# Raw state-space parameters loaded from GpSimd's queue, their tables begun in the first quarter of the first MLP, and the last gate made inside the second MLP

## The chip, the cores and the metric

One Trainium2 chip, of which the kernel uses one core. The metric is the device time of one execution in microseconds. The core's engines are TensorE (PE: matmuls; PEld is its weight loads), VectorE (DVE), ScalarE (ACT), GpSimd (POOL) and SyncE (SP); each runs its own instructions in a fixed order and waits on semaphores for the others. TensorE's clock has two levels, 1.2 and 2.4 GHz; the granted clock is its mean as a share of the higher one.

## The reference

Two layers on x of 256 tokens and 2048 channels. Each has a token mixer and a squared-ReLU MLP of 8192 hidden channels; before each stands an RMS norm with shift and scale, behind each a gated residual add. The six vectors of a layer come from the conditioning vector c.

```python
for i in range(2):
    mod = silu(c) @ ada_w[i] + ada_b[i]
    sh1, sc1, g1, sh2, sc2, g2 = split(mod, 6)
    h = rmsnorm(x, ln1_g[i]) * (1 + sc1) + sh1
    y = stick_breaking_mixer(h, ...) if i == 0 else s5_mixer(h, ...)
    x = x + g1 * y
    h = rmsnorm(x, ln2_g[i]) * (1 + sc2) + sh2
    a = relu(h @ mlp_w1[i])
    x = x + g2 * ((a * a) @ mlp_w2[i])
```

The S5 mixer runs 128 groups of 16 channels through a complex diagonal state space of 64 states. From lambda, dt, B and C (b_re, b_im, c_re, c_im) it needs discretised matrices and powers of the diagonal: the tables of this text.

## The kernel before

Every large product is f32 and split in two: a weight tile of 512 KB is loaded into w by SP's queue (L128), ACT rounds it to wh (L130), DVE computes the rest wl = w - wh (L132), and PE makes three products, 24 matmuls per tile in the MLP. w, wh and wl have three buffers each, so PE can go on for at most three tiles when DVE stops. After each tile the program calls `tick`, which counts `now`, makes a share (`rate`) of a unit of the vectors from c, and runs what `at` has put down for this tick. A unit is a load of 512 KB into adaw (L265) and two DVE instructions (L350, for the first of a sum L348). `pace` sets the rate so that a vector is done after so many ticks, `drain` finishes it at once.

The first MLP has four quarters of 64 tiles: 32 of w1, then 32 of w2. `between` is called in the first quarter after 16 tiles, `ready` in the last. While this MLP runs, the S5 tables are made: `s5_tables` puts down, for each of eight groups gi, `s5_raws` (loads b_re and b_im into the tile W and c_re, c_im into C, each with one buffer), `s5_powers` (PE turns C over, L896; ACT copies it to CT, L899; POOL, L903 to L917, and DVE, L921 to L926, multiply; POOL's queue stores W to pw in DRAM, L927) and two `s5_turns` (POOL multiplies turns, L744 to L848, and stores it to rot, L849). The S5 mixer loads pw and rot again.

PE and POOL run in the order in which the program is written; the order on SP, ACT and DVE is made by the scheduler when the program is built, and is fixed then. The last vector, g2 of layer 1, stands at the end of the queue of units, and the second MLP reads it in its first residual, 36 tiles in.

```python
w = self.wp.tile([P, a, b], F32, name="w", bufs=self.nw)
nc.sync.dma_start(w, src)
h = self.wp.tile([P, a, b], F32R, name="wh", bufs=self.nh)
nc.scalar.activation(h, w, AF.Copy)
l = self.wp.tile([P, a, b], F32R, name="wl", bufs=self.nh)
nc.vector.tensor_tensor(l, w, h.bitcast(F32), op=OP.subtract)
```

Of the kernel before, what the change touches and what calls it, by code (L numbers as in the profile page):

```python
# [56 lines left out]
class Trunk:  # L57
# [424 lines left out]
            nc.scalar.activation(r[:, j, :S], r[:, j, :S], func, bias=r[:, j, S:])  # L482

    @with_exitstack
    def mlp(ctx, self, layer, nxt=None, last=False, between=None, middle=None):
        nc = self.nc
        w1, w2 = self.i["mlp_w1"][layer], self.i["mlp_w2"][layer]
        hH, hL = self.h()
# [4 lines left out]
        for q in range(4):  # L493
            aH = rp.tile([P, NB, S], F32R, name="aH", bufs=1)
            aL = rp.tile([P, NB, S], F32R, name="aL", bufs=1)
            if q == 0:
# [6 lines left out]
                    nc.scalar.activation(halves[g], acc[:, :, :S + 1], AF.Copy)  # L503
                if between:
                    between()
            if q == 1 and middle:
                middle()
            for g in range(8):
                if 8 * q + g < ahead:
                    acc = self.gemm_cols(w1, q * 2048 + g * 256, hH, hL, 8, 16)  # L510
# [2 lines left out]
                else:  # L513
                    src = self.gemm_cols(w1, q * 2048 + g * 256, hH, hL)
# [297 lines left out]
    def s5_tables(self, tmp):  # L812
        v = self.recorder = Recorder(self.nc.vector)
        lo = tmp.tile([P, 2, 64, 8], F32, name="s5lo")
        hi = tmp.tile([P, 2, 64, 8], F32, name="s5hi")
        t, c2, s2 = (tmp.tile([P, 64], F32, name=n) for n in ("s5t", "c2", "s2"))
        pc, ps = self.s5["pc"], self.s5["ps"]
        tb = tmp.tile([P, 64, 4], F32, name="s5tb")
        for tab in (lo, hi):
            v.memset(tab[:, 0, :, 0:1], 1.0)  # L820
            v.memset(tab[:, 1, :, 0:1], 0.0)
            for n in (1, 2, 4):
                B = lambda a: a[:, :, None].to_broadcast([P, 64, n])
                self.cmul(v, tab[:, 0, :, n:2 * n], tab[:, 1, :, n:2 * n],
                          tab[:, 0, :, 0:n], tab[:, 1, :, 0:n], B(pc), B(ps), tb[:, :, :n])
                self.cmul(v, c2, s2, pc, ps, pc, ps, t)
                pc, c2 = c2, pc
                ps, s2 = s2, ps
        self.rot = [self.dram.tile([P, 3, 4 * 64], F32, name="rot%d" % bi) for bi in range(16)]
        self.pw = [self.dram.tile([P, 2, 2, 4, 8, 16], F32, name="pw%d" % gi) for gi in range(8)]  # L830
        for gi in range(8):
            self.at(28 + 16 * gi, self.s5_raws, tmp, gi)
            self.at(32 + 16 * gi, self.s5_powers, tmp, gi)
            for bi in (2 * gi, 2 * gi + 1):
                self.at(36 + 8 * bi, self.s5_turns, tmp, lo, hi, bi)

    def s5_turns(self, tmp, lo, hi, bi):
        nc = self.nc
# [30 lines left out]
    def s5_raws(self, sp, gi):  # L869
        nc, i = self.nc, self.i  # L870
        g0 = 16 * gi
        W = sp.tile([P, 2, 2, 4, 8, 16], F32, name="W")
        Ec = W[:, 0]
        C = sp.tile([P, 2, 2, 2, 64], F32, name="C", bufs=1)
        for c, n in enumerate(("s5_b_re", "s5_b_im")):
            nc.sync.dma_start(Ec[:, c, 0], i[n][0, g0:g0 + 16].rearrange("(q a) p c -> (a p) q c", a=2))
        for c, n in enumerate(("s5_c_re", "s5_c_im")):
            src = i[n][0, g0:g0 + 16].rearrange("(b g) c p -> (g c) b p", b=2)
            for dup in range(2):
                nc.sync.dma_start(C[:, c, :, dup], src)  # L880
        self.raw = W, C

    def s5_powers(self, sp, gi):
# [244 lines left out]
    def run(self):  # L1128
        nc = self.nc
# [31 lines left out]
        M = lambda i: bool(0 >> i & 1)  # L1161
        self.sums = self.ctx.enter_context(self.tc.tile_pool(name="sums", bufs=1))
        mid = [self.ada_vec(1, 4, M(4)), self.ada_vec(1, 3, M(5))]
        nxt = [self.ada_vec(1, 1, M(1)), self.ada_vec(1, 0, M(2))]
        self.queue += [self.ada_vec(0, 5, M(0))] + nxt + [self.ada_vec(1, 2, M(3))] + mid + [self.ada_vec(1, 5, M(6))]
        self.dram = self.ctx.enter_context(self.tc.tile_pool(name="dram", bufs=1, space=bass.MemoryType.DRAM))
        self.rate = 1.0

        def between():
            self.drain(gates[1])  # L1170
            self.shifts(8, 16, 0, 1)
            for kb in range(8, 16):
                self.fold(kb, 0, 1)
            self.rate = 0.6

        stp = ExitStack()

        def params():
            tmp = stp.enter_context(self.tc.tile_pool(name="s5t", bufs=1))
            self.s5_tables(tmp)  # L1180

        def ready():
            self.recorder.play(None)
# [2 lines left out]
            self.open_h(self.pers)  # L1186
            self.shifts(0, 16, 1, 0)

        self.mlp(0, nxt=ready, between=between, middle=params)
        self.dump("x2")  # L1190
        self.rate = 0.35
        self.s5_mixer(mid)
        self.dump("x3")
        self.logexp()
        self.rate = 1.0
        self.mlp(1, last=True)


# [26 lines left out]
```

## Time and profile before

| | |
|---|---|
| median of 3 runs | 2492.97 us (2491.97 to 2493.75) |
| profiled execution | 2488.38 us |
| its span, first to last instruction | 2486.6 us |
| busy: PE, DVE, ACT, POOL | 2374.3, 1830.0, 1207.1, 255.6 us |
| mean granted TensorE clock | 0.986 |
| DMA, mean | 252 GB/s |

The busy time is a sum over stages that have different limits: attention (to about 490 us), the first MLP (to 1341), the S5 mixer (to about 1730) and the second MLP. A wait in the profile names the instruction that waited, the one that released it, the time in total, the times and the longest. Idle time of an engine that nobody waits for costs nothing.

### The profile page before, as it was taken

To read this page: it belongs to the slowest core of one execution; us is meant where nothing else is said; L and a number is where in the kernel's file an instruction comes from. 1 tells how busy PE (TensorE), PEld (TensorE's weight loads), DVE (VectorE), ACT (ScalarE), POOL (GpSimd) and SP (SyncE) were. 2 spreads that over 40 slices of the span, in tenths; PEclk is the share of its full clock that TensorE was granted. 3 is DMA by queue.
4 is the path that set the end of the run, shared out by engine and by line. 5 is a ranking of instruction groups with operands and counts; after the bars stand their busy time and mean duration, and the time that the engine had idled before them with its cause. 6 is when DMAs were issued, how large, how long until landed. Compare 5 with 4: busy or idle time off the path is not lost.

```text
span 2486.6 us, 48432 instructions
## 1 busy us (share of the span) xinstructions
PE 2374.3 (95%) x19843; PEld 2234.8 (90%) x19843; DVE 1830.0 (74%) x2479; ACT 1207.1 (49%) x1806; POOL 255.6 (10%) x292
## 2 busy tenths in 40 slices
PE   7999999999999888988999999999999999999998
PEld 4776789899999778888999998999999999999998
DVE  5699999999888878787797699658555555555543
ACT  4534875355444234433546676444543543543543
POOL 0000100000003444454400000000000000000000
PEclk9999999999999989999999999999999999999999
DMA  9898899999998888888898577768555655655654
GB/s 337 301 309 301 289 315 320 334 309 317 320 306 286 274 269 276 262 287 282 279 312 304 179 240 228 230 186 280 177 181 186 184 183 185 185 184 184 185 184 140
DMA packets 503058, 627.28 MB, mean 252 GB/s; under 512 B 44434, under 2 KB 374580, under 8 KB 500532
## 3 DMA queue, kind: packets, MB, share of 16 engines
q1 hardware_dynamic: 499776, 609.31, 75.1%
q0 software_dynamic: 2432, 14.68, 1.5%
q8 instruction: 155, 2.54, 0.4%
q14 instruction: 67, 0.55, 0.1%
q10 hardware_dynamic: 628, 0.21, 0.0%
HBM read 607.34 MB, written 16.78 MB: 251 GB/s over the span
## 4 chain that ended last, share of the span: by engine, by line
PE 58%; DVE 13%; issue 10%; DMA 9%; POOL 7%; ACT 2%; SPq 0%; ACTq 0%; DVEq 0%; POOLq 0%
PE acc L159 14%; PE acc L161 14%; PE acc L160 14%; DMA adaw<-in_ada_w 5%; DVE wl L132 4%; PE acc L145 3%; PE acc L146 3%; PE acc L147 3%; DVE adacc L350 3%; DMA rot<-turns 2%; DVE adsums L350 2%; DMA w<-in_mlp_w 2%; PE mp L291 1%; PE mp L322 1%; ACT wh L130 1%
## 5 line engine op out<-in xcount | busy, mean ns | idle before, releaser
L130 ACT ACTIVATE wh<-w 128x1024 fp32r<-128x1024 f32 x736 | 777.5, 1058 | 1052.9 <-PE acc L161 544.6
L132 DVE TENSOR_TENSOR wl<-w,wh 128x1024 fp32r<-128x1024 f32 x736 | 914.9, 1245 | 409.3 <-ACT wh L130 408.3
L159 PE MATMUL acc<-hH,wl 128*128 128x258 f32 (+1 forms) x2816 | 808.1, 287 | 33.7 <-DVE wl L132 32.2
L161 PE MATMUL acc<-hH,wh 128*128 128x258 f32 (+1 forms) x2816 | 799.5, 284 | 0.0
L160 PE MATMUL acc<-hL,wh 128*128 128x258 f32 (+1 forms) x2816 | 798.0, 283 | 0.5 <-DVE hL L122 0.5
L159 PE MATMUL acc<-aH,wl 128*128 128x256 f32 x2048 | 587.4, 287 | 39.1 <-DVE wl L132 38.4
L160 PE MATMUL acc<-aL,wh 128*128 128x256 f32 x2048 | 581.6, 284 | 0.0
L161 PE MATMUL acc<-aH,wh 128*128 128x256 f32 x2048 | 581.6, 284 | 0.0
L159 PEld LDWEIGHTS acc<-hH,wl 128*128 128x128 f32 x2816 | 535.9, 190 | 48.7 <-DVE wl L132 38.3
L160 PEld LDWEIGHTS acc<-hL,wh 128*128 128x128 f32 x2816 | 536.6, 191 | 0.7 <-DVE hL L122 0.7
L161 PEld LDWEIGHTS acc<-hH,wh 128*128 128x128 f32 x2816 | 535.1, 190 | 0.0
L159 PEld LDWEIGHTS acc<-aH,wl 128*128 128x128 f32 x2048 | 391.0, 191 | 48.5 <-DVE wl L132 47.1
L160 PEld LDWEIGHTS acc<-aL,wh 128*128 128x128 f32 x2048 | 391.1, 191 | 0.0
L161 PEld LDWEIGHTS acc<-aH,wh 128*128 128x128 f32 x2048 | 391.0, 191 | 0.0
L350 DVE SCALAR_TENSOR_TENSOR adacc<-adaw,cond,adacc 128x512 f32<-128x512 f32 x390 | 296.9, 763 | 22.5 <-DMA adaw<-in_ada_w 19.2
L350 DVE SCALAR_TENSOR_TENSOR adsums<-adaw,cond,adsums 128x512 f32<-128x512 f32 x270 | 216.1, 802 | 30.5 <-DMA adaw<-in_ada_w 26.5
L145 PE MATMUL acc<-wh,hL 128*128 128x512 f32 x384 | 156.8, 408 | 5.8 <-ACT wh L130 3.1
L146 PE MATMUL acc<-wl,hH 128*128 128x512 f32 x384 | 153.6, 400 | 3.4 <-DVE wl L132 3.3
L147 PE MATMUL acc<-wh,hH 128*128 128x512 f32 x384 | 152.6, 398 | 0.0
L145 PEld LDWEIGHTS acc<-wh,hL 128*128 128x128 f32 x384 | 73.3, 191 | 32.3 <-issue 13.7
L146 PEld LDWEIGHTS acc<-wl,hH 128*128 128x128 f32 x384 | 72.9, 190 | 21.2 <-DVE wl L132 6.3
L147 PEld LDWEIGHTS acc<-wh,hH 128*128 128x128 f32 x384 | 73.0, 190 | 17.0
(288 smaller groups left out, 2068.9 us busy)
## 6 DMA issues: line engine op xcount, KB each, us to landing
w<-in_mlp_w SPq DMA_DIRECT2D x512, 512.0 KB, 3.9
adaw<-in_ada_w SPq DMA_DIRECT2D x384, 512.0 KB, 5.8
w<-in_sb_w_in SPq DMA_DIRECT2D x96, 512.0 KB, 5.5
w<-in_s_w_glu SPq DMA_DIRECT2D x64, 512.0 KB, 3.9
w<-in_sb_w_out SPq DMA_DIRECT2D x32, 512.0 KB, 5.6
w<-in_s_w_in SPq DMA_DIRECT2D x32, 512.0 KB, 4.6
pw<-W POOLq DMA_DIRECT2D x8, 1024.0 KB, 4.2
W<-pw SPq DMA_DIRECT2D x8, 1024.0 KB, 6.7
```

Of the source, the lines that this page charges most:

```text
L130: nc.scalar.activation(h, w, AF.Copy)
L132: nc.vector.tensor_tensor(l, w, h.bitcast(F32), op=OP.subtract)
L145: nc.tensor.matmul(o, aL(kb)[:, s], H[:, kk], start=(kb == k0), stop=False)
L146: nc.tensor.matmul(o, aH(kb)[:, s], L[:, kk], start=False, stop=False)
L147: nc.tensor.matmul(o, aH(kb)[:, s], H[:, kk], start=False, stop=(kb == k1 - 1))
L159: nc.tensor.matmul(o, L[:, kk, s], aH(kb), start=(kb == k0), stop=False)
L160: nc.tensor.matmul(o, H[:, kk, s], aL(kb), start=False, stop=False)
L161: nc.tensor.matmul(o, H[:, kk, s], aH(kb), start=False, stop=(kb == k1 - 1))
L291: nc.tensor.matmul(st["bank"][32 * kk:32 * kk + 32], self.cond32[:, 4 * t + kk], pair[kk // 2][:, kk % 2], start=(t == 0), stop=(t == 3))
L322: nc.tensor.matmul(st["bank"][32 * i:32 * i + 32], self.ones[:, 0:32], acc, start=True, stop=True)
L350: nc.vector.scalar_tensor_tensor(acc, wt[:, kk], c, acc, op0=OP.mult, op1=OP.add)
```

## The change

The six loads of `s5_raws` go from SP's queue to POOL's. `params`, which opens the tables, is called at the end of `between`, 16 tiles into the first MLP, and no longer at the start of its second quarter; a group now takes 22 ticks, with the first turns ahead of the powers, where it took 16, with both turns behind. The rate of the units in the first MLP is 0.5 after `between`, and was 0.6. The last vector leaves the queue and joins it just before the second MLP, at a pace of 29 ticks.

```diff
--- before.py
+++ after.py
@@ -482,7 +482,7 @@
             nc.scalar.activation(r[:, j, :S], r[:, j, :S], func, bias=r[:, j, S:])
 
     @with_exitstack
-    def mlp(ctx, self, layer, nxt=None, last=False, between=None, middle=None):
+    def mlp(ctx, self, layer, nxt=None, last=False, between=None):
         nc = self.nc
         w1, w2 = self.i["mlp_w1"][layer], self.i["mlp_w2"][layer]
         hH, hL = self.h()
@@ -503,8 +503,6 @@
                     nc.scalar.activation(halves[g], acc[:, :, :S + 1], AF.Copy)
                 if between:
                     between()
-            if q == 1 and middle:
-                middle()
             for g in range(8):
                 if 8 * q + g < ahead:
                     acc = self.gemm_cols(w1, q * 2048 + g * 256, hH, hL, 8, 16)
@@ -829,10 +827,11 @@
         self.rot = [self.dram.tile([P, 3, 4 * 64], F32, name="rot%d" % bi) for bi in range(16)]
         self.pw = [self.dram.tile([P, 2, 2, 4, 8, 16], F32, name="pw%d" % gi) for gi in range(8)]
         for gi in range(8):
-            self.at(28 + 16 * gi, self.s5_raws, tmp, gi)
-            self.at(32 + 16 * gi, self.s5_powers, tmp, gi)
-            for bi in (2 * gi, 2 * gi + 1):
-                self.at(36 + 8 * bi, self.s5_turns, tmp, lo, hi, bi)
+            o = 30 + 22 * gi
+            self.at(o, self.s5_raws, tmp, gi)
+            self.at(o + 1, self.s5_turns, tmp, lo, hi, 2 * gi)
+            self.at(o + 9, self.s5_powers, tmp, gi)
+            self.at(o + 14, self.s5_turns, tmp, lo, hi, 2 * gi + 1)
 
     def s5_turns(self, tmp, lo, hi, bi):
         nc = self.nc
@@ -873,11 +872,11 @@
         Ec = W[:, 0]
         C = sp.tile([P, 2, 2, 2, 64], F32, name="C", bufs=1)
         for c, n in enumerate(("s5_b_re", "s5_b_im")):
-            nc.sync.dma_start(Ec[:, c, 0], i[n][0, g0:g0 + 16].rearrange("(q a) p c -> (a p) q c", a=2))
+            nc.gpsimd.dma_start(Ec[:, c, 0], i[n][0, g0:g0 + 16].rearrange("(q a) p c -> (a p) q c", a=2))
         for c, n in enumerate(("s5_c_re", "s5_c_im")):
             src = i[n][0, g0:g0 + 16].rearrange("(b g) c p -> (g c) b p", b=2)
             for dup in range(2):
-                nc.sync.dma_start(C[:, c, :, dup], src)
+                nc.gpsimd.dma_start(C[:, c, :, dup], src)
         self.raw = W, C
 
     def s5_powers(self, sp, gi):
@@ -1162,22 +1161,24 @@
         self.sums = self.ctx.enter_context(self.tc.tile_pool(name="sums", bufs=1))
         mid = [self.ada_vec(1, 4, M(4)), self.ada_vec(1, 3, M(5))]
         nxt = [self.ada_vec(1, 1, M(1)), self.ada_vec(1, 0, M(2))]
-        self.queue += [self.ada_vec(0, 5, M(0))] + nxt + [self.ada_vec(1, 2, M(3))] + mid + [self.ada_vec(1, 5, M(6))]
+        self.queue += [self.ada_vec(0, 5, M(0))] + nxt + [self.ada_vec(1, 2, M(3))] + mid
+        last = self.ada_vec(1, 5, M(6))
         self.dram = self.ctx.enter_context(self.tc.tile_pool(name="dram", bufs=1, space=bass.MemoryType.DRAM))
         self.rate = 1.0
+
+        stp = ExitStack()
+
+        def params():
+            tmp = stp.enter_context(self.tc.tile_pool(name="s5t", bufs=1))
+            self.s5_tables(tmp)
 
         def between():
             self.drain(gates[1])
             self.shifts(8, 16, 0, 1)
             for kb in range(8, 16):
                 self.fold(kb, 0, 1)
-            self.rate = 0.6
-
-        stp = ExitStack()
-
-        def params():
-            tmp = stp.enter_context(self.tc.tile_pool(name="s5t", bufs=1))
-            self.s5_tables(tmp)
+            self.rate = 0.5
+            params()
 
         def ready():
             self.recorder.play(None)
@@ -1186,13 +1187,14 @@
             self.open_h(self.pers)
             self.shifts(0, 16, 1, 0)
 
-        self.mlp(0, nxt=ready, between=between, middle=params)
+        self.mlp(0, nxt=ready, between=between)
         self.dump("x2")
         self.rate = 0.35
         self.s5_mixer(mid)
         self.dump("x3")
         self.logexp()
-        self.rate = 1.0
+        self.queue.append(last)
+        self.pace(29, last)
         self.mlp(1, last=True)
```

DVE, about the first two multiplications of the second group's b (L921 and L922 before, L920 and L921 in the change; a line number of the change is one lower from there on, and `x2` means two equal instructions). Before, the wl ahead of them is the seventh after the transposes of the first group:

```order
L418 SCALAR_TENSOR_TENSOR xT<-half_6164,mod_79,xT 128x256 x2
L132 TENSOR_TENSOR wl<-w,wh 128x1024
L921 TENSOR_TENSOR w_8972<-W,powers 128x384
L922 TENSOR_TENSOR w_8973<-W,powers 128x384
L132 TENSOR_TENSOR wl<-w,wh 128x1024
L923 TENSOR_TENSOR W<-w_8972,w_8973 128x384
L350 SCALAR_TENSOR_TENSOR adsums<-adaw,cond,adsums 128x512
L924 TENSOR_TENSOR w_8972<-W,powers 128x384
L132 TENSOR_TENSOR wl<-w,wh 128x1024
L925 TENSOR_TENSOR w_8973<-W,powers 128x384
```

In the change, again seven tiles after the first group's transposes:

```order
L132 TENSOR_TENSOR wl<-w,wh 128x1024
L920 TENSOR_TENSOR w_7745<-W,powers 128x384
L921 TENSOR_TENSOR w_7746<-W,powers 128x384
L350 SCALAR_TENSOR_TENSOR adsums<-adaw,cond,adsums 128x512
L922 TENSOR_TENSOR W<-w_7745,w_7746 128x384
L350 SCALAR_TENSOR_TENSOR adsums<-adaw,cond,adsums 128x512
L132 TENSOR_TENSOR wl<-w,wh 128x1024
L923 TENSOR_TENSOR w_7745<-W,powers 128x384
L924 TENSOR_TENSOR w_7746<-W,powers 128x384
```

The two instructions keep their distance of seven tiles to the transposes of the group before, and the next wl stands behind them; in the change L922 (formerly L923) and the two instructions of a unit (L350) stand between.

POOL, from the store of the first group's W. Before, two sets of turns follow (the first is shown), and then the next group's powers:

```order
L927 DMA pw_7140<-W 128x2048
L744 TENSOR_TENSOR turnq<-s5lo,s5hi 128x256
L745 TENSOR_TENSOR turns<-s5lo,s5hi 128x256
L746 TENSOR_TENSOR turns<-turnq,turns 128x256
L747 TENSOR_TENSOR turnq<-s5lo,s5hi 128x256
L748 TENSOR_TENSOR turns<-s5lo,s5hi 128x256
L749 TENSOR_TENSOR turns<-turnq,turns 128x256
L848 TENSOR_SCALAR turns<-turns 128x256
L849 DMA rot_7124<-turns 128x768
```

In the change one set follows, and behind its store the loads of the next group:

```order
L926 DMA pw_5475<-W 128x2048
L742 TENSOR_TENSOR turnq<-s5lo,s5hi 128x256
L743 TENSOR_TENSOR turns<-s5lo,s5hi 128x256
L744 TENSOR_TENSOR turns<-turnq,turns 128x256
L745 TENSOR_TENSOR turnq<-s5lo,s5hi 128x256
L746 TENSOR_TENSOR turns<-s5lo,s5hi 128x256
L747 TENSOR_TENSOR turns<-turnq,turns 128x256
L847 TENSOR_SCALAR turns<-turns 128x256
L848 DMA rot_5460<-turns 128x768
L875 DMA W<-in_s_b_re 128x8x16
L875 DMA W<-in_s_b_im 128x8x16
L879 DMA C<-in_s_c_re 128x2x64 x2
```

The loads of b (L875) and C (L879) moved into this queue, behind the store of W and a set of turns.

SP, about the loads of the second group's b. Before:

```order
L128 DMA w<-in_mlp_w 128x4x256
L265 DMA adaw<-in_ada_w 128x2x512
L128 DMA w<-in_mlp_w 128x4x256
L876 DMA W<-in_s_b_re 128x8x16
L128 DMA w<-in_mlp_w 128x4x256
L876 DMA W<-in_s_b_im 128x8x16
L265 DMA adaw<-in_ada_w 128x2x512
L128 DMA w<-in_mlp_w 128x4x256
L265 DMA adaw<-in_ada_w 128x2x512
```

At the same distance from the first group's transposes in the change:

```order
L128 DMA w<-in_mlp_w 128x4x256
L265 DMA adaw<-in_ada_w 128x2x512
L128 DMA w<-in_mlp_w 128x4x256
L265 DMA adaw<-in_ada_w 128x2x512
L128 DMA w<-in_mlp_w 128x4x256
L265 DMA adaw<-in_ada_w 128x2x512
L128 DMA w<-in_mlp_w 128x4x256
L265 DMA adaw<-in_ada_w 128x2x512
```

The two loads of W between the weights are gone; weights and units alternate.

## Rows read from the trace of the kernel before

**Rows 1.** The page: TensorE's busy time, its share of the span and its instructions.
```profile
PE 2374.3 (95%) x19843; PEld 2234.8 (90%) x19843; DVE 1830.0 (74%) x2479; ACT 1207.1 (49%) x1806; POOL 255.6 (10%) x292
```

**Rows 2.** Windows: stretch, length, busy us (x instructions) per engine, clock, DMA share, GB/s.
```profile
541.00:781.00 240.00, 235.94 (x1947) 232.47 (x1946) 213.06 (x296) 120.79 (x151) 0.00 (x0) 1.00 0.94 315
781.00:1197.00 416.00, 355.01 (x2742) 344.86 (x2740) 327.04 (x373) 149.32 (x177) 197.43 (x210) 0.93 0.84 273
1197.00:1341.00 144.00, 138.85 (x1139) 135.33 (x1138) 125.23 (x167) 71.41 (x100) 28.84 (x30) 1.00 0.91 302
1414.00:1514.00 100.00, 100.00 (x1709) 91.81 (x1707) 88.73 (x132) 70.79 (x147) 0.00 (x0) 1.00 0.74 238
1660.00:1730.00 70.00, 70.00 (x587) 69.03 (x586) 58.64 (x83) 31.91 (x41) 0.00 (x0) 1.00 0.84 270
1900.00:2000.00 100.00, 100.00 (x837) 100.00 (x836) 52.33 (x51) 48.87 (x59) 0.00 (x0) 1.00 0.60 182
```

**Rows 3.** The line L896 (transposes of C): ns min/median/max, first and last start.
```profile
L896 PE MATMUL mp<-ident,C x32: 270/272/274, 781.0 to 1197.4; 128*128 128x128 f32 x32
```

**Rows 4.** Timeline of PE, first and fifth group: start us, us, instruction.
```profile
781.04 0.60 PE L896 MATMUL mp<-ident,C 128*128 128x128 f32 x4
...
1023.89 0.60 PE L896 MATMUL mp<-ident,C 128*128 128x128 f32 x4
```

**Rows 5.** Waits of SP's queue, 781 to 1197: us in total, times, longest.
```profile
SPq L876 <- DMA pw<-W: 73.1, 7, 12.3
```

**Rows 6.** Waits, all engines, 781 to 1197 us.
```profile
PEld acc L159 <- DVE wl L132: 69.1, 36, 7.0
```

**Rows 7.** Timeline of POOL, first and fifth group.
```profile
784.64 0.51 POOL L903 TENSOR_TENSOR t<-CT,fr 128x128 f32<-128x128 f32 x1 [389.78 <-ACT CT L899]
...
798.64 0.74 POOL L927 DMA_DIRECT2D pw<-W  x1 [0.31 <-POOL W L917]
...
806.33 0.62 POOL L849 DMA_DIRECT2D rot<-turns  x1 [0.31 <-POOL turns L848]
...
1026.03 0.63 POOL L903 TENSOR_TENSOR t<-CT,fr 128x128 f32<-128x128 f32 x1 [20.30 <-ACT CT L899]
...
1048.00 0.62 POOL L849 DMA_DIRECT2D rot<-turns  x1 [0.30 <-POOL turns L848]
```

**Rows 8.** Timeline of SP, first group.
```profile
803.57 0.37 SPq L876 DMA_DIRECT2D W<-in_s_b_re  x1
```

**Rows 9.** Timeline of DVE, first group; in brackets the idle time before and its releaser.
```profile
802.15 1.64 DVE L132 TENSOR_TENSOR wl<-w,wh 128x1024 fp32r<-128x1024 f32 x1
805.82 0.56 DVE L921 TENSOR_TENSOR w<-W,powers 128x384 f32<-128x384 f32 x1 [2.03 <-DMA W<-in_s_b_re]
809.16 0.56 DVE L922 TENSOR_TENSOR w<-W,powers 128x384 f32<-128x384 f32 x1 [2.78 <-DMA W<-in_s_b_im]
809.64 1.22 DVE L132 TENSOR_TENSOR wl<-w,wh 128x1024 fp32r<-128x1024 f32 x1
...
812.82 0.75 DVE L350 SCALAR_TENSOR_TENSOR adsums<-adaw,cond,adsums 128x512 f32<-128x512 f32 x1 [1.50 <-DMA adaw<-in_ada_w]
```

**Rows 10.** The lines L927, L876 and L128: DMA issues, ns min/median/max.
```profile
L927 POOL DMA_DIRECT2D pw<-W x8: 603/603/738, 798.6 to 1212.8; - x8
...
L876 SPq DMA_DIRECT2D W<-in_s_b_re x8: 367/368/458, 711.4 to 1161.5; - x8
L876 SPq DMA_DIRECT2D W<-in_s_b_im x8: 498/574/578, 711.9 to 1162.5; - x8
...
L128 SPq DMA_DIRECT2D w<-in_mlp_w x512: 367/368/1473, 480.1 to 2465.3; - x171
```

**Rows 11.** Windows of the instructions on adaw alone (DVE's part).
```profile
541.00:1341.00 800.00, 0.00 (x0) 0.00 (x0) 262.95 (x331) 0.97 0.88 291
1197.00:1341.00 144.00, 0.00 (x0) 0.00 (x0) 48.80 (x64) 1.00 0.91 302
1660.00:1730.00 70.00, 0.00 (x0) 0.00 (x0) 23.15 (x32) 1.00 0.84 270
```

## The prediction

> **What bounds the kernel now.** I read the page first: TensorE (PE) is busy 95% of the span [rows 1], so the question is where the rest is lost. The table of windows answers it [rows 2]. A weight tile is 24 matmuls. In the second MLP 837 matmuls pass in 100 us, 100/(837/24) = 2.867 us per tile: PE's own pace. In the first MLP, 541 to 781 us holds 1947 matmuls, or 81.1 tiles in 240 us, 2.96 each; 1197 to 1341 us holds 1139, or 47.5 tiles, 3.03 each; together 2.99. Between them, 781 to 1197 us, it is the stage of the state-space tables that falls out: the granted clock is 0.93 and PE loses 61 us of busy time there alone. The four transposes of C open each group of the tables. Eight groups start between 781.0 and 1197.1 us (the last of the 32 transposes at 1197.4) [rows 3], so seven intervals of 16 tiles took 416 us, 59.4 us each. PE needs 16 x 2.867 + 0.6 (the transposes) = 46.5 us. That is 13 us lost per interval, some 90 us in all.
>
> Then I asked who waits. SP's queue lists 73.1 us in seven waits, up to 12.3 us: the load of b_re into W waits for the store of the group before, because W has one buffer [rows 5]. Behind it stand the weights. This is what the move to GpSimd's queue (POOL) removes. But PE itself waits for wl, which VectorE (DVE) writes [rows 6], and DVE has a wait of its own for the same loads.
>
> Take the first interval and count from its transposes at T0 = 781.04 [rows 4]. POOL starts on the powers at 784.64, issues the store of W at 798.64 and the store of the next turns at 806.33 [rows 7]. SP, held until the store has landed, issues b_re at 803.57 [rows 8]. DVE has written its 7th wl after T0 at 803.8 and now meets, in its own fixed order, the two multiplications that read b_re and b_im (L921, L922). They start at 805.82 and 809.16, and only behind them comes the next wl, 809.64 to 810.86 [rows 9]: T0 + 29.8. From there 9 tiles of 2.867 us, 25.8 us, lead to the next T0. 29.8 + 25.8 = 55.6 of the 59.4 us that an interval takes in the mean. Read in the same way, the seven restarts come 27.0 to 30.8 us after T0, 29.2 in the mean. So an interval is 29.2 + 25.8 + 4.4, and the 4.4 hold the half clock after each gap and weights that SP sent late. The restart is what counts: PE can be fast or slow up to it, since it has only the tiles whose wl stand ahead of L921.
>
> **The change, part by part.** *The loads move to POOL.* SP's 73 us of waits go, and its 48 issues. The Trainium skill (DMA: Bandwidth & Descriptors, section Issuing engines are not separate DMA queues) says that another issuing engine saves only the sequencer's time to issue, since all DMAs share 16 engines. By that alone the sum would be 0: 48 issues of about 0.47 us on a queue with slack. The trace differs in that SP's loss was a wait and not issue time [rows 5].
>
> Freed SP time helps only if DVE doesn't wait, so I ask when the data are there now. DVE's order still has L920 and L921 (formerly L921 and L922) seven tiles behind the transposes of the group before, as the order shows for the second group and as I counted for all seven. POOL runs in program order: powers, store of W, one set of turns, its store, and only then the loads of the next group. With rows of the kernel before:
> - T0 to POOL's start: 3.6 us in the first interval, 2.1 in the fifth, where the weights were in time [rows 4, 7]. I take 2.2, as SP won't be late.
> - POOL's start to the store of the next turns: 21.7 and 22.0 us [rows 7]; 21.3 in the mean of seven. Its issue: 0.6.
> - Issue of b_re and b_im on POOL: no row shows it. POOL's stores take 0.60 to 0.74 us each with 128 rows [rows 10]; b has 1024 runs of 64 bytes. Lower bound 0.6; if the cost went with the runs, 8 x 0.6 = 4.8. SP's issue of b takes 1.0 to 1.6 times its issue of a weight tile [rows 10], so the near row says little growth: 0.9 each, 1.8 for both.
> - Landing: b_re was used 2.25 us after SP began its issue in the first interval [rows 8, 9], 0.4 of it issue: 2.0.
> - The second multiplication 0.6, then DVE's work up to the end of the next wl: in the second group L350, L922, L350 and L132, 0.75 + 0.56 + 0.75 + 1.22 = 3.3 us [rows 9]; 2.6 in the mean of the seven orders.
>
> Sum: 2.2 + 21.3 + 0.6 + 1.8 + 2.0 + 0.6 + 2.6 = 31.1 us after T0, against 29.2. PE has weights until 0.6 + 7 x 2.867 = 20.7 us after T0, so I expect a gap of about 10 us in each interval, seven times, as now. SP's wait lay under DVE's wait; taking it away uncovers nothing.
>
> *The tables are spread.* An interval is now 22 ticks: 31.1 + 15 x 2.867 + 4.4 = 78.5 us, seven of them 549.5. The kernel before spent on as many tiles 416 + 42 x 2.99 = 541.5. So +8. The number of gaps is the same, and begun in the first quarter, they only stand earlier. What is queued behind the waiting DVE instruction is every wl, and PE waits for those; behind POOL's loads only tables stand, for which it has 22 x 2.867 = 63 us per group and, today, 197.43/7 = 28 us of work [rows 2].
>
> *Rate 0.5 in place of 0.6.* 240 ticks x 0.1 = 24 gate units leave the first MLP. Some 165 units pass through DVE there, two instructions each [rows 11]; outside the gaps they cost at most 2.99 - 2.867 = 0.12 us per tile x 240 / 165 = 0.18 us each: -4 us. They land, with the last vector's 32, in S5, the GLU and the start of the second MLP.
>
> *The last gate inside the second MLP.* In SP's order 36 of its units and of those before it now stand in the last 48 tiles of the GLU, 0.75 per tile, and 8 in the first 16 tiles of the MLP. With 16 units in 24.5 tiles the GLU ran at 70/24.5 = 2.86 us per tile [rows 2, 11]: free. With 32 in 47.5 tiles the end of the first MLP paid 0.16 per tile [rows 2, 11]. Between 0 and 0.16 x 48 = 8 I take +3, by the GLU's own row. S5, where PE is busy throughout and DVE 89% [rows 2], and the start of the second MLP: +2, between 0 and 10.
>
> Sum: +8 - 4 + 3 + 2 = +9 us. The profiled execution took 2488.4 us, 4.6 below the median of the runs, so 2497.4 there and **2502 us** against 2492.97.
>
> **The rivals.**
> - *Faster: SP's wait was the stall.* If weights never stop, an interval is 22 x 2.867 + 0.6 = 63.7 us, 446 for seven, 95 less than 541.5, where the sum above has 8 more: about 2399 us. For it speaks that 73 us at SP are as long as PE's loss. It needs b_im in SBUF some 18 us after T0, so that the next wl is done at 20.7; but the store that must free W is only issued 17.6 us after T0 [rows 4, 7]. Chance 0.08.
> - *Somewhat faster:* the gaps stay, but SP has filled its buffers meanwhile and the 4.4 us fall to 1. 7 x 3.4 = 24 less: about 2478. Chance 0.14.
> - *POOL is slow to issue.* At 4.8 us per load both come 7.8 us later, 7 x 7.8 = 55: about 2557. The Trainium skill (SBUF — State Buffer, section SBUF: two separate sides) warns that DMAs from GpSimd are held up when VectorE holds the port they share, 620 ns becoming 3100. By its figure, an estimate, the loads would be 2 x 2.2 x 7 = 31 us later in sum: about 2533. The trace has not shown it: the slowest of POOL's stores of W took 0.74 us beside a busy DVE [rows 10], and DVE stands still when these loads are issued. Chance 0.12.
> - *S5 suffers:* in the change's orders 32 units stand in S5's 32 tiles on SP, 13 before, and part of the loads of the tables stand behind them. If none of the 19 more is hidden, DVE needs 19 x 2 x 0.75 = 28 us for them [rows 9], 8 of which lie in its idle 11% there: about 2522. Chance 0.08.
> - *Nothing changes:* the later loads and the freed queue cancel, 2493. Chance 0.06.
>
> **How the numbers follow.** The forecast itself has 0.52, with restarts 30 to 34 us after T0, which is 2502 - 7 x 1.1 = 2494 to 2502 + 7 x 2.9 = 2522. Of it 0.14 lies within 0.2% of the time before (5 us, about what a measurement of this kernel can tell). Slower: 0.38 + 0.12 + 0.08 = 0.58. Same: 0.14 + 0.06 = 0.20. Faster: 0.08 + 0.14 = 0.22. The range, 2470 to 2550, leaves out the free stall and the slow end of POOL's issues.
>
> **What would show it.** Right: SP's list has no wait for the store of W; DVE's list has one for b_re of 10 us and more, seven times, larger in sum than now; PE's gaps begin about 21 us after the transposes and end about 31 us after them; transposes 78 us apart; a granted clock that still falls in this stage. Wrong: transposes 64 to 70 us apart, no wait at DVE, a clock of 1.00. POOL's issue of b in the trace decides the size. If DVE reached L920 with the data landed, the whole forecast falls.

## The result, and the profile after

The changed kernel takes 2523.94 us (median of 4 runs, 2520.14 to 2524.86); the kernel before took 2493.36 beside it. The ratio is 1.0115, with a 95% interval of 1.0096 to 1.0134: about 30 us slower. Predicted were 2502 us, with a range of 2470 to 2550, and a chance of 0.58 that the change is slower. The direction and the mechanism held; of the 30 us the prediction had 9.

The windows of the changed kernel answer to [rows 2]. The columns are the same: stretch, length, busy us (x instructions) of PE, PEld, DVE, ACT and POOL, granted clock, DMA share, GB/s.

```profile
546.00:665.00 119.00, 115.75 (x952) 114.14 (x951) 110.96 (x169) 60.14 (x78) 8.34 (x8) 1.00 0.92 303
665.00:1233.00 568.00, 476.52 (x3764) 465.49 (x3763) 410.38 (x472) 210.51 (x251) 225.62 (x252) 0.92 0.77 254
1900.00:2000.00 100.00, 100.00 (x841) 100.00 (x840) 52.12 (x54) 43.01 (x47) 0.00 (x0) 1.00 0.59 183
```

In the second MLP PE still passes 841 matmuls in 100 us. The loss stands where it stood before, in the stage of the tables, which now begins at 665 us: PE is idle for 91 of its 568 us, at a clock of 0.92. Seven intervals lie between the first and the last transposes (answers to [rows 3]):

```profile
L895 PE MATMUL mp<-ident,C x32: 270/272/273, 664.9 to 1233.1; 128*128 128x128 f32 x32
```

That is 568 / 7 = 81.1 us per interval, where the prediction had 78.5. The waits of this stretch (us in total, times, longest), first of all engines and then of SP's queue, answer to [rows 5, 6]:

```profile
PEld acc L159 <- DVE wl L132: 92.2, 37, 14.0
...
DVE w L920 <- DMA W<-in_s_b_re: 70.2, 7, 11.9
```

```profile
SPq L128 <- DVE wl L132: 423.6, 150, 15.9
```

SP's list has no wait for the store of W any more; 73.1 us are gone from it, and but for 1.2 us SP now waits only for buffers that DVE frees. DVE waits seven times for b_re, 70.2 us in sum, 10 each. In the kernel before, between 781 and 1197 us, it waited less than half of that:

```profile
DVE w L921 <- DMA W<-in_s_b_re: 31.0, 7, 7.3
```

PE waits for wl behind it. These are the signs that the prediction had named for its being right; only its two times were short, 78 us per interval and gaps that end 31 us after the transposes.

POOL's timeline in the second group (transposes at 749.96) and the fourth (916.27) shows the restart being set (answers to [rows 7, 8]):

```profile
755.65 0.77 POOL L902 TENSOR_TENSOR t<-CT,fr 128x128 f32<-128x128 f32 x1 [51.02 <-ACT CT L898]
...
770.95 0.61 POOL L926 DMA_DIRECT2D pw<-W  x1 [0.30 <-POOL W L916]
...
777.97 0.61 POOL L848 DMA_DIRECT2D rot<-turns  x1 [0.30 <-POOL turns L847]
778.59 0.91 POOL L875 DMA_DIRECT2D W<-in_s_b_re  x1
779.48 0.89 POOL L875 DMA_DIRECT2D W<-in_s_b_im  x1
...
918.41 0.63 POOL L902 TENSOR_TENSOR t<-CT,fr 128x128 f32<-128x128 f32 x1 [44.79 <-ACT CT L898]
...
938.17 0.90 POOL L875 DMA_DIRECT2D W<-in_s_b_re  x1 [0.52 <-DMA pw<-W]
```

And DVE in the second group (answers to [rows 9]):

```profile
771.13 1.64 DVE L132 TENSOR_TENSOR wl<-w,wh 128x1024 fp32r<-128x1024 f32 x1
782.58 0.56 DVE L920 TENSOR_TENSOR w<-W,powers 128x384 f32<-128x384 f32 x1 [9.81 <-DMA W<-in_s_b_re]
783.05 0.55 DVE L921 TENSOR_TENSOR w<-W,powers 128x384 f32<-128x384 f32 x1
783.52 1.11 DVE L350 SCALAR_TENSOR_TENSOR adacc<-adaw,cond,adacc 128x512 f32<-128x512 f32 x1
784.56 1.64 DVE L132 TENSOR_TENSOR wl<-w,wh 128x1024 fp32r<-128x1024 f32 x1
```

The next wl ends at 786.2, 36.2 us after the transposes. Over the seven groups the restarts (ends of the next wl, from the transposes) are 37.1, 36.2, 36.7, 30.4, 37.1, 30.7 and 35.8: two clusters. Between the transposes and the restart DVE worked on 6, 5.5, 4, 0.5, 5, 0 and 3.5 units of the vectors: the two early restarts are the groups that had next to none. The fourth group's b is issued 21.9 us after its transposes, the second group's 28.6.

### The profile page after: what moved, and what is told of

Its sections match the earlier page's. It is cut to its first block, busy times and chain, and to the rows that moved or that the text cites. A ratio compares the mean times of both kernels' runs of the same rounds, so it can differ in the third digit from the quotient of the medians.

```text
span 2523.1 us, 48416 instructions
## 1 busy us (share of the span) xinstructions
PE 2376.2 (94%) x19843; PEld 2236.4 (89%) x19843; DVE 1833.1 (73%) x2479; ACT 1208.5 (48%) x1806; POOL 292.2 (12%) x340
## 4 chain that ended last, share of the span: by engine, by line
PE 42%; DVE 5%; DMA 4%; issue 2%; ACT 1%; SPq 0%; DVEq 0%; ACTq 0%
PE acc L159 13%; PE acc L161 12%; PE acc L160 12%; DMA adaw<-in_ada_w 3%; DVE wl L132 2%; DVE adsums L350 1%; PE mp L997 1%; PE mp L1022 1%; PE mp L982 1%; PE mp L959 1%; PE mp L952 0%; DVE xT L418 0%; DVE adacc L350 0%; PE mp L967 0%; DMA W<-pw 0%
## 5 line engine op out<-in xcount | busy, mean ns | idle before, releaser
L350 DVE SCALAR_TENSOR_TENSOR adacc<-adaw,cond,adacc 128x512 f32<-128x512 f32 x390 | 296.7, 762 | 22.2 <-DMA adaw<-in_ada_w 18.4
L350 DVE SCALAR_TENSOR_TENSOR adsums<-adaw,cond,adsums 128x512 f32<-128x512 f32 x270 | 213.5, 792 | 22.1 <-DMA adaw<-in_ada_w 19.1
L145 PEld LDWEIGHTS acc<-wh,hL 128*128 128x128 f32 x384 | 73.7, 192 | 32.4 <-issue 12.8
L147 PEld LDWEIGHTS acc<-wh,hH 128*128 128x128 f32 x384 | 73.4, 191 | 17.1
```

Of the source, the lines that this page charges most:

```text
L145: nc.tensor.matmul(o, aL(kb)[:, s], H[:, kk], start=(kb == k0), stop=False)
L147: nc.tensor.matmul(o, aH(kb)[:, s], H[:, kk], start=False, stop=(kb == k1 - 1))
L350: nc.vector.scalar_tensor_tensor(acc, wt[:, kk], c, acc, op0=OP.mult, op1=OP.add)
```

## The experiments

Each was run on one chip beside the kernel before, whose median lay between 2490.6 and 2496.1 us. Ratios are to that kernel, with a 95% interval. "Restart" is read as in the prediction: the end of the first wl behind the waiting instructions, from the transposes, mean of seven.

**The loads alone.** In the kernel before, `nc.sync` becomes `nc.gpsimd` in the six loads of `s5_raws`.

> The kernel before, with only the six loads moved to GpSimd's queue. They stand there behind the store of W and both sets of turns. SP's wait of 73.1 us in seven goes. Theory (DVE's wait decides, and on POOL the loads come late): POOL starts 2.2 us after the transposes, stores the first turns at 23.5, waits some 5.5 us for that store and needs some 7.2 us for the second turns, then 0.6 + 1.8 for the issues, 2.0 to land, 0.6 and 3 on DVE: a restart at about 44 us in place of 29.2, an interval of 44 + 25.8 + 4 = 74 in place of 59.4, and 2493 + 7 x 14.5 = about 2595 (2565 to 2615). Rival, SP's wait for the store of W was the stall: about 90 us less than before, 2400. Rival, the loads' queue doesn't matter: 2493.

Measured: 2546.39 us, ratio 1.0203 (1.0183 to 1.0223). The restart is 43.4 us, as expected; the interval is 66.2 and not 74, in the main because in DVE's order of this kernel the two multiplications had moved about 1.7 tiles further back, so that fewer tiles were left behind them: 1.7 x 2.867 = 4.9 of the 7.8 us. Right in sign and mechanism, half the size. SP's wait for the store is gone from its list, DVE's wait has trebled, and the kernel is slower:

```profile
DVE w L921 <- DMA W<-in_s_b_re: 96.8, 7, 16.7
```

SP's wait alone was not the stall.

**The loads back on SP**, in the changed kernel:

```diff
-            nc.gpsimd.dma_start(Ec[:, c, 0], ...
+            nc.sync.dma_start(Ec[:, c, 0], ...
...
-                nc.gpsimd.dma_start(C[:, c, :, dup], src)
+                nc.sync.dma_start(C[:, c, :, dup], src)
```

> The changed kernel, with the six loads back on SP's queue; the tables stay spread and early, the gates as changed. Theory (the restart is set by the queue that the loads stand in): on SP they wait for the store of W alone and no longer for the turns and their store behind it, so the restart goes from 34.9 back to about 29 us after the transposes, as in the kernel before, while SP's waits return and cost some of the 1.2 us that the remainder had fallen by: 2524 - 7 x (5.9 - 1.2) = about 2491 (2478 to 2502). Rival, the spread and the gates cost the 31 us: 2515 to 2525. Rival, contention of GpSimd's own loads: the same 2491, but then POOL's instructions are faster in this run.

Measured: 2491.73 us, ratio 0.9989 (0.9977 to 1.0001). The restart is 28.7, the interval 76.3. SP's wait is back, DVE's is smaller:

```profile
SPq L875 <- DMA pw<-W: 72.7, 7, 11.8
```

```profile
DVE w L920 <- DMA W<-in_s_b_re: 46.4, 7, 8.6
```

So tables that are spread and early cost nothing in themselves; the whole loss hangs on the queue in which the loads stand.

**The gates alone**, in the kernel before: rate 0.5, and the last vector queued ahead of the second MLP with `pace(29, last)`.

> The kernel before, with only the change to the gates: rate 0.5 in place of 0.6 in the first MLP, the last vector put in the queue ahead of the second MLP at a pace of 29 ticks. Loads and tables as before. Theory of the prediction: -4 us in the first MLP, +5 in S5, the GLU and the start of the second MLP, so +1, 2494 to 2497 beside a kernel before of 2493 to 2496; within 0.2% of it. Rival, the gates cost the 31 us of the change or a large part of them: 2510 or more.

Measured: 2494.39 us, ratio 0.9997 (0.9987 to 1.0007). No difference, as expected, and by DVE's timeline the two parts came as predicted too: the first MLP took 849.1 us against 853.2, and what follows it 7 us more.

**b in a tile of its own**, in the changed kernel:

```diff
+        B = sp.tile([P, 2, 8, 16], F32, name="B", bufs=2)
...
+        v.tensor_tensor(Ec[:, 0, 1:], e1, ai, op=OP.mult)
...
+        g_.tensor_copy(Ec[:, :, 0], B)
```

B is loaded 14 ticks earlier; DVE's multiplications read b from it (e0 and e1 are views of B), and POOL copies it into W ahead of the store.

> The changed kernel, with b in a tile of its own (two buffers, loaded 14 ticks earlier on GpSimd's queue, copied into W there). The loads of b then wait for nothing; what DVE still waits for is W itself, which its second multiplication now writes, so it is held until the store of the group before has landed. Theory (DVE, waiting for W in its fixed order, holds wl): that store is issued 17.1 us after the transposes in the changed kernel and takes some 4.9 us to land (rows of before: 798.64 to 803.57), so the restart comes at 17.1 + 4.9 + 0.6 + 3 = 25.6 us in place of 34.9, an interval is 81.1 - 9.3 = 71.8 us, and the time 2524 - 7 x 9.3 = about 2459 (2440 to 2475); DVE's wait is then for the store of pw and no longer for b. Rival, the spread tables and the gates cost the time and not the wait for b: about 2524. Rival, GpSimd's queue is what holds everything up: it has as much work as before and one copy more, so 2524 or more.

Measured: 2536.02 us, ratio 1.0163 (1.014 to 1.0185). The expectation of 2459 failed, though its first half held. Two waits of DVE in the stage:

```profile
DVE W L926 <- DMA pw<-W: 55.4, 7, 9.8
...
DVE w L925 <- DMA B<-in_s_b_re: 32.7, 6, 9.2
```

The timeline of the third group (transposes at 834.5) shows both:

```profile
857.10 0.56 DVE L926 TENSOR_TENSOR W<-B,powers 128x384 f32<-128x384 f32 x1 [4.71 <-DMA pw<-W]
...
859.10 1.22 DVE L132 TENSOR_TENSOR wl<-w,wh 128x1024 fp32r<-128x1024 f32 x1
...
873.12 0.56 DVE L925 TENSOR_TENSOR w<-B,powers 128x384 f32<-128x384 f32 x1 [6.50 <-DMA B<-in_s_b_re]
```

The first wl behind the store ends 25.8 us after the transposes in this group, 27.7 in the mean (expected 25.6). But L925, free of W now, stands three wl further on, for the group after next, and reaches its place before that load, which POOL issues at 869.07. The wait moved with the load. That the scheduler places an instruction by an arrival that it reckons too early fits this, but is argued and not shown.

**The same in the kernel before**, with B loaded by SP and one buffer.

> The kernel before, with b in a tile of its own, loaded by SP as now, and copied into W by POOL. SP then waits for no store of W (73.1 us go), b is there early, and DVE is held only by its first write into W, until the store of the group before has landed. Theory (the wait that counts is DVE's for W): the store is issued 17.6 us after the transposes and was seen to take some 4.9 us in the first group; restart at 17.6 + 4.4 + 0.6 + 1.2 + 1.5 = about 25.3 in place of 29.2 us, so 7 x 3.9 = 27 us less, and some of the remainder: about 2465 (2445 to 2475). Rival, SP's wait was the stall: with no wait at SP the intervals fall to 46.5 to 48 us, 2410 to 2420. Rival, neither matters: 2493.

Measured: 2499.44 us, ratio 1.0016 (1.0005 to 1.0026). A miss: 2465 were expected. With one buffer SP had to wait for POOL's copy out of B, which I had overlooked:

```profile
SPq L877 <- POOL W L927: 59.7, 7, 11.3
```

The restart is 27.2 in place of 29.2, the interval 59.8; this run says little more than that a wait was exchanged for another.

**b multiplied on POOL**, in the changed kernel, the loads where they were:

```diff
-        v.tensor_tensor(u1, e0, ar, op=OP.mult)
+        g_.tensor_tensor(u1, e0, ar, op=OP.mult)
...
-        v.tensor_tensor(Ec[:, 1, 1:], u1, u2, op=OP.add)
+        g_.tensor_tensor(Ec[:, 1, 1:], u1, u2, op=OP.add)
```

> The changed kernel, with the six multiplications and sums on b made by POOL in place of DVE. The loads stay where they are and come no earlier; POOL has some 8 us more work per group (six instructions of 1.3 us), 40 of about 64 us. Theory (the loss is DVE standing still in its fixed order with every wl behind it): with no DVE instruction that waits for b, PE never lacks wl for long, an interval falls from 81.1 to 22 x 2.867 + 0.6 = 63.7 us by PE's pace, or to 22 x 2.96 + 0.6 = 65.7 by the pace of the stretch without tables, and the time to 2524 - 7 x 15.4 to 17.4 = 2402 to 2416, say 2412 (2395 to 2430); the granted clock stays at 1.00 in this stage. Rival, the late loads or POOL's queue themselves hold the group up: 2524 or more. Rival, the spread and the gates: 2524.

Measured: 2477.06 us, ratio 0.9927 (0.9908 to 0.9946): 47 us less than the changed kernel, though its loads come later still, 35.1 us after the transposes in the mean against 25.1. PE's waits for wl, up to 14.0 us each in the changed kernel, are now short (665 to 1179 us):

```profile
PEld acc L159 <- DVE wl L132: 54.2, 44, 3.3
```

The cause of the gaps is thereby shown. But 110 were expected: the interval is 73.4 and not 65. Its windows, an interval with units (second) and one without (sixth), tell more:

```profile
743.00:822.00 79.00, 69.26 (x534) 67.09 (x533) 68.18 (x70) 36.41 (x48) 43.74 (x42) 0.96 0.91 299
...
1041.00:1105.00 64.00, 64.00 (x542) 64.00 (x541) 34.49 (x33) 24.96 (x26) 41.11 (x42) 1.00 0.75 235
```

Without units an interval takes 64 us and PE is never idle; with some 18 it takes 79. DVE and POOL in the second interval, side by side:

```profile
765.47 1.29 POOL L921 TENSOR_TENSOR w<-W,powers 128x384 f32<-128x384 f32 x1
766.83 1.34 POOL L922 TENSOR_TENSOR W<-w,w 128x384 f32<-128x384 f32 x1
768.24 1.70 POOL L923 TENSOR_TENSOR w<-W,powers 128x384 f32<-128x384 f32 x1
```

```profile
767.22 2.03 DVE L132 TENSOR_TENSOR wl<-w,wh 128x1024 fp32r<-128x1024 f32 x1
770.27 1.21 DVE L350 SCALAR_TENSOR_TENSOR adsums<-adaw,cond,adsums 128x512 f32<-128x512 f32 x1
```

A wl takes 1.22 us alone and 2.03 here. Between 500 and 1350 us of this run, the wl with no POOL work beside them took 1.22 in the mean (174 of them), those with POOL at work for over 80% of their time 1.63 (66); a unit's L350 0.75 (190) and 1.08 (90). POOL's 128x256 products took 0.66 with DVE idle (11) and 1.09 with DVE at work for over 80% of their time (69). Two explanations remained: DVE and POOL slow each other, or DMA (0.91 of its time in the second interval) slows both.

One instruction tells them apart. L418, the residual add, reads either two inputs from SBUF (half and xT) or one from SBUF and one from PSUM, the memory that PE writes (acc). Its groups between 665 and 1179 us (busy us, mean ns of one, idle us before):

```profile
L418 DVE SCALAR_TENSOR_TENSOR xT<-half,mod,xT 128x256 f32<-128x256 f32 x16 | 11.6, 762 | 0.2
L418 DVE SCALAR_TENSOR_TENSOR xT<-acc,mod,xT 128x256 f32<-128x256 f32 x16 | 7.1, 477 | 2.7 <-PE acc L161 2.7
```

In the traces of all fourteen kernels here (500 to 1350 us) the form with half takes 0.48 us without POOL (114) and 0.80 beside POOL (99), the form with acc 0.48 and 0.47 (291 and 123, none above 0.49). Busy DMA would not spare one of the two. What the slowing costs the kernel is the question of the next runs.

**The units made even.** The pool `sums` is left out; with partial sums in two buffers the units can't run far ahead. First in the changed kernel, then with b on POOL.

```diff
-        self.sums = self.ctx.enter_context(self.tc.tile_pool(name="sums", bufs=1))
```

> The changed kernel, with the vectors' partial sums kept in two buffers in place of six, so that the units can no longer run 48 ahead of the tables: by the order they come 8 in every 16 tiles, where they came 50 in a row and then none for 24 tiles. As many units in all. In the changed kernel the groups with units beside them restarted 35.8 to 37.1 us after the transposes, the two without at 30.4 and 30.7. Theory (a unit beside POOL's table work makes DVE and POOL slower, and that is the part by which the restart was under-estimated): by the order two groups have units beside POOL's work in full and three in part, so a mean restart of 30.5 + 6 x 3.5 / 7 = 33.5 in place of 34.9, and 2524 - 10 = about 2514 (2502 to 2522). Rival, the spread of 30 to 37 us is POOL's own: no relation to the units, 2524. Rival, the fewer buffers cost more than the evenness gives: over 2524.

Measured: 2509.9 us, ratio 1.0065 (1.0047 to 1.0082). Restart 32.4, interval 78.4.

> The kernel with b multiplied on POOL (2477 us), with the units made even in the same way. In that kernel no DVE instruction waits for b, yet its intervals take 63.1 us without units and 77 to 79 with 18 to 20 units beside POOL's work; wl there takes up to 2.0 us in place of 1.22 and a unit's instructions 1.2 to 1.5 in place of 0.75 while POOL works. Theory (what is left of the loss is DVE and POOL slowing each other where a unit stands on nearly every tile): 11 even units per interval, some half beside POOL, at 0.85 us each and the others at 0.2, make 64 + 5.5 x 0.85 + 5.5 x 0.2 = 69.5 us in place of 73.4, so 7 x 3.9 = 27 less: about 2450 (2435 to 2468). Rival, DMA is the bound there (0.92 of its time): the same bytes in fewer pauses, so up to 7 x 5 less as well, but then wl and the units' instructions are not slower beside POOL. Rival, neither: 2477.

Measured: 2458.06 us, ratio 0.9851 (0.9837 to 0.9864), interval 71.5. Both times lie in the ranges expected.

**The units apart from POOL's work, or beside it.** In the last kernel, 8 units per group in two phases:

```diff
+        self.at(28, self.units, 8 / 22)
+        self.at(208, self.units, 0.8)
```

`units` sets the rate. This is the run with units apart; beside has 10 in place of 28.

> The kernel with even units and b on POOL (2458 us), with 8 units per group in place of 11 while the tables are made (rate 8/22), and 0.8 behind them; by the order the 8 stand on the last 8 tiles ahead of a group's transposes, where POOL has finished. Theory (DVE and POOL slow each other: wl 1.22 us alone and 1.6 beside POOL, a unit's instructions 0.75 and 1.08): with 14 tiles beside POOL at PE's pace of 2.867 and 8 at 3.05, as in the stretches with units and no POOL work, an interval takes 0.6 + 40.1 + 24.4 = 65.1 us in place of 71.5, and some 10 units more behind the tables cost 2 us: 2458 - 45 + 2 = about 2416 (2408 to 2435). Rival, DMA or the number of units sets the pace: three units fewer per interval at what a unit cost on average, (71.5 - 63.7) / 11 = 0.7 us, so 7 x 2.1 = 15 less, 2443, and the same in the run with the units beside POOL. Rival, no effect: 2458.

> The same kernel with the rate of 8/22 begun 18 ticks earlier, so that the 8 units of a group stand by the order on the first 8 tiles behind the transposes, all beside POOL's table work. As many units per group, as many bytes, the same instructions. Theory (DVE and POOL slow each other): each unit costs some 0.8 us there, so an interval takes 63.7 + 8 x 0.8 = 70 us where the run with the units apart takes 65, 7 x 5 = 35 us more than that run: about 2450 (2440 to 2462). Rival, DMA or the number of units sets the pace: within 8 us of the run with the units apart.

Measured, on one chip: apart 2429.96 us, ratio 0.9741 (0.9705 to 0.9777); beside 2455.58, ratio 0.9845 (0.9814 to 0.9876). Both lie in the ranges expected; the rival that only the number of units counts had both at 2443. Intervals 64.9 and 68.0. The parting is not complete: 2 to 2.5 of a group's 8 units still stand beside POOL's instructions in the first run, and 4.5 to 5.5 in the second. The windows of the whole stage, apart:

```profile
662.00:1116.00 454.00, 453.86 (x3746) 446.57 (x3745) 351.66 (x359) 208.56 (x249) 294.31 (x294) 1.00 0.88 280
```

and beside:

```profile
664.00:1140.00 476.00, 458.98 (x3749) 448.62 (x3747) 361.42 (x358) 210.96 (x253) 304.90 (x294) 1.00 0.83 266
```

As many instructions on DVE (but one) and POOL in both, and 22 us between the stages; DVE and POOL are each busy 10 us longer when they meet. With the units apart PE is busy for 453.86 of 454 us, at a DMA share of 0.88: DMA was not the bound. "Apart" is the fastest kernel of the study, some 63 us below the one before.

**The change with units apart**: the last kernel, with b back on DVE.

> The changed kernel (b multiplied on DVE, loads on GpSimd's queue) with even units, 8 per group, standing apart from POOL's work as in the run above. DVE's wait for b is back, but no unit stands beside POOL's work up to the restart. Theory (the restart was under-estimated by what units beside POOL add): all restarts come 30 to 31.5 us after the transposes, as in the two groups of the changed kernel that had no units, an interval takes 31 + 15 x 2.867 + 3 = 77 us, and the time is 2510 (even units) - 7 x 1.4 = about 2500 (2490 to 2510), near what was predicted for the change. Rival, the late restart comes from POOL's issue and landing of b alone: 34 to 35 us after the transposes as before, 2515 to 2525.

Measured: 2520.0 us, ratio 1.0097 (1.0063 to 1.0131). The restart, 31.0 in the mean (29.1 to 32.3), and the interval, 77.7, came about as expected. Even so the time came out 20 us over: the stage gained 24 us over the changed kernel, and the units that it no longer makes there were made behind it, most of them in the GLU: by DVE's timeline its 64 tiles took 238.4 us with 64 units, against 218.5 with 42 in the changed kernel.

Beside the fastest kernel, which has the same units per group and the multiplications on POOL, this run also shows the whole price of DVE's wait: 2520.0 against 2429.96 us on one chip, 90 us, of which 7 x (77.7 - 64.9) = 90 are in this stage.

**The loads of the fastest kernel back on SP.**

> The kernel with the units apart and b on POOL (2430 us), with the six loads back on SP's queue. Nothing on DVE waits for b. On SP the loads of b stand behind 9 weight tiles counted from the transposes, so SP reaches them some 17 us after the transposes (PE is then in the seventh tile, and SP three ahead); the store of W is issued 24.7 us after the transposes there and lands some 4.9 us later. Theory (with DVE's wait gone, a wait in SP's queue is no longer covered): SP stands still for some 12 us, the next weight is issued at 24.7 + 4.9 + 1.0 = 30.6 and its wl is done at about 30.6 + 2.5 + 1.1 + 1.2 = 35.4 us, where PE has run dry at 0.6 + 9 x 2.867 = 26.4: 9 us per interval, 7 x 9 = 63, so about 2493 (2478 to 2505). Rival, SP's waits are never on the path: 2430.

Measured: 2517.21 us, ratio 1.01 (1.0075 to 1.0125). Now SP's wait decides:

```profile
SPq L880 <- DMA pw<-W: 105.3, 7, 16.6
```

Expected were 2493. The restart is where it was expected (35.0 to 35.7 us, but 40.2 in the first group), and PE ran nine tiles ahead of the gap, as expected. What the expectation left out is what follows a gap: it counted the 9 us of idle time alone, but the granted clock of this stage (the third number from the end) is 0.93, where it is 1.00 in the fastest kernel, and the interval became 76.9 and not 74:

```profile
667.00:1205.00 538.00, 469.52 (x3747) 461.03 (x3745) 327.70 (x360) 211.17 (x254) 227.33 (x252) 0.93 0.74 238
```

## Why the prediction was right, and where its size came from

*The mechanism.* That DVE's wait in its fixed order sets the restart, and that SP's wait lay under it, is shown from three sides: with SP's wait gone and DVE's left, the kernel is slower by 2%; with the loads back on SP the loss is gone; and with no such instruction on DVE the long gaps are gone though the loads come later. The rival "SP's wait was the stall" falls. It was right about another kernel: where nothing on DVE waits, the move to POOL is worth some 89 us (ratios 1.01 and 0.9741). Why the move failed here is that it came alone.

How close the two waits lay can be read from ACT in the kernel before, first group (transposes at 781.04):

```profile
798.61 1.06 ACT L130 ACTIVATE wh<-w 128x1024 fp32r<-128x1024 f32 x1 [2.28 <-DMA w<-in_mlp_w]
808.21 1.06 ACT L130 ACTIVATE wh<-w 128x1024 fp32r<-128x1024 f32 x1 [8.54 <-DMA w<-in_mlp_w]
```

The first is the wh of the tile with which PE restarts: it was done 10 us before DVE came to it, so DVE alone held that tile. The second belongs to the next tile, whose weights stood behind SP's wait. It was done 28.2 us after the transposes, 29.2 in the mean of the seven groups, just when the restart came. An estimate from these rows: had DVE not waited, SP's wait would have let PE restart at 29.2 + 1.2 = 30.4, one tile later. Each wait hid the other; by this estimate, which no run tests in the kernel before, the removal of either alone gains little.

*The step that was off* is the restart: 31.1 us predicted, 34.9 measured, 7 x 3.8 = 27 us. Term by term, from the transposes (T0): T0 to POOL 3.2 (2.2 predicted); POOL to the store of the turns 20.9 (21.3); from there to the loads 1.0 (0.6); issue of the first load, landing and the multiplications up to the end of the second 6.0 (1.8 + 2.0 + 0.6 = 4.4); DVE to the end of the next wl 3.7 (2.6). POOL's issue, the unknown that decided the size, was taken at 0.9 and is 0.90 to 0.91. The term of POOL's work held; the four others were sized too small by 4.1 us together. What makes the difference is shown by the run with units apart: without units beside the tables the restart is 31.0 in the mean, 3.9 less, and its terms are 2.7, 19.2, 0.6, 5.0 and 3.5. Units beside the tables slow DVE and POOL. The rows of before held such units too, so the term of POOL's work, 21.3, had them in it; the term of DVE's work was added up from lengths without POOL beside them (0.75 and 1.22 us). That the 31.0 meets the predicted 31.1 is chance in part: POOL's work is 2.1 us shorter there and the other terms 2.0 longer. The forecast's inner band, restarts of 30 to 34 us and 2494 to 2522 us, was just missed, at 34.9 and 2524.

*The remainder* of 4.4 us fell to 3.2 (81.1 - 34.9 - 15 x 2.867), 8 us less in sum. The rival that SP fills its buffers while DVE stands was so partly right, beside the forecast and not in its place. Together the stage came 18 us above the prediction's +8.

*The gates* were worth nothing alone, as predicted. In the profiled executions the rest of the first MLP came out 1 us shorter (predicted 4) and S5, the GLU and the start of the second MLP 6 longer (predicted 5). Another 5 us of the difference of the two spans lie ahead of the first MLP, in code that is the same in both; that is scatter between executions: the end of the first wl of that MLP lies between 488.8 and 494.5 us in all the traces.

*The rivals of POOL.* The slow issue (4.8 us each) did not come, nor did the stretch to five times: the slowest load of b took 1.08 us to issue. But the warning of the Trainium skill (SBUF — State Buffer, section SBUF: two separate sides), that VectorE and GpSimd share a port pair, was met in another place, in the lengths of the instructions. It says that an operation of VectorE with two inputs in SBUF and one of GpSimd that reads SBUF exclude each other for the whole instruction. The traces agree: L418 is slowed with two inputs in SBUF and not with one (0.80 and 0.47 us beside POOL), and 2.03 us for a wl is its own 1.22 and 0.81 of waiting, about one of POOL's 128x384 products with DVE idle (0.84). The pair of runs with units apart and beside, which moves two to three of a group's units, shows a price, 25.6 us for the whole kernel where 35 were expected.

*Left open:* by what rule the scheduler places the instructions that wait. Its choice was read from the order of each kernel, and in two runs (the loads alone, b in a tile of its own) it had moved.

## What to carry to other kernels

Two engines can wait for one transfer, and one wait can hide the other: before a load is moved off a queue, look for the instruction that consumes it and for what stands behind that one in its own order. Here the move cost 30 us with that wait in place and was worth some 89 without it. A load put behind compute work on GpSimd's queue is as late as that work, and a consumer that stands ahead of it in a fixed order stalls all behind it. Spread side work so that VectorE's share doesn't meet GpSimd's: here the same instructions in another phase were worth 1%.

## What was not expected of the hardware

An issue on GpSimd's queue took 0.90 us for b (1024 runs of 64 bytes), 0.71 for C (256 runs of 256 bytes) and 0.61 for the stores with 128 rows, so here it grew little with the runs. The landing of b came later than from SP's queue in the kernel before: 3.9 us from the start of the issue in the median, against 2.6.

```profile
L875 POOL DMA_DIRECT2D W<-in_s_b_re x8: 903/906/1078, 495.9 to 1179.2; - x8
L875 POOL DMA_DIRECT2D W<-in_s_b_im x8: 890/896/907, 497.0 to 1180.1; - x8
...
DMA to landing us min/median/max: 2.9/3.9/7.3
```

VectorE and GpSimd slowed each other by a third to two thirds (wl, the units' L350, L418 with half; GpSimd's 128x256 products), but an instruction of VectorE with one of its two inputs in PSUM was not slowed at all (L418 with acc, 0.47 us beside GpSimd). Neither engine's list of waits names it: it shows only as longer instructions.
